# An encoder layer on one core: three side steps a place later, one run of loads on another queue

## The chip, the cores and the metric

The kernel runs on one core of a Trainium2 chip. The metric is the device time of one execution, in microseconds (us). One execution was also recorded by the hardware profiler; its rows give for each instruction the start from the beginning of the span, how long it took and, where the engine stood idle before it, what ended the idle time. PE is the matrix engine, DVE the vector engine, ACT the scalar engine, POOL is GpSimd, and SP is the engine that issues nearly all transfers.

## The reference

```python
mod = jax.nn.silu(c) @ w_ada + b_ada
shift, scale, gate = jnp.split(mod, 3, axis=-1)
h = rmsnorm(x, pre_g) * (1.0 + scale[:, None]) + shift[:, None]
proj = h @ w_in
q, k, v, gate_a, u, gate_p = jnp.split(proj, SPLIT_POINTS, axis=-1)
y_a = windowed_gqa(q, k, v, rel_table, sink) * jax.nn.silu(gate_a)
y_p = multiscale_pool(u, w_pool_grp, pool_scale) * jax.nn.silu(gate_p)
g_a, g_p = jnp.split(jax.nn.sigmoid(h @ w_merge + b_merge), N_BRANCHES, axis=-1)
merged = g_a * (y_a @ w_br_attn) + g_p * (y_p @ w_br_pool)
x = x + gate[:, None] * rmsnorm(merged @ w_out, post_g)
```

x has 1024 rows of 2048 values, w_in is 2048 x 4608, w_merge 2048 x 4096, both branch weights 1024 x 2048, w_out 2048 x 2048; everything is 32-bit floating point.

## The kernel before, in words

**Products.** Each 32-bit operand is split into a high part, which ACT copies (`whi` for weights, line 96), and a low part, which DVE subtracts (`wlo`, line 97). A product is three matmul passes: high by high, high by low, low by high. The big matrix products go through `strassen`: a pair of 128 output rows by 1024 tokens is computed with seven such products of sums of blocks, into three PSUM banks X, Z and V, in the order X<-B11, V<-T3, Z<-T2, X<-B21, V<-T4, Z<-T1, Z<-B22. B11, T3, T2, B21, T4, T1, B22 are seven prepared forms of the moving operand. Between the products ACT copies X into the next Z (line 285), copies Z out as u4 (line 302) and X or Z as c (line 320), and DVE prepares the next weights: sums of blocks of `raw` (lines 114, 117), and `ws`.

**Pairs and side steps.** `run` takes a pair through its seven pieces and, behind some of them, takes one step off a queue `side`. All that is not the main product is such a step: column sums for the modulation, norms, loads and transposes of x, the gate, the pooling, preparation of the next operand. `strassen` is a generator, and the end of a pair (its Z<-B22) is run inside the next pair (`late`, `flush`). The weights `raw` of a pair are loaded about a pair ahead. The order in which an engine takes its instructions follows from the order in which the steps are written, save where a scheduler moves one; `keep` fixes an instruction in the order.

**The four places.**

- *Ramp, from 85 to 112 us.* `modulation(3, …)` sums the fourth group of modulation columns: four steps of GEMV matmuls, whose result ACT copies into `acc` (line 519); a fifth step, `columns`, transposes `acc` with four matmuls into the bank PM (line 480), which DVE reduces (line 482) and turns into `modc` (lines 487, 490). With `modc` ACT and DVE modulate the tiles xT (lines 567, 568) that the next moving operands are made of. `late_sums` says at which of thirteen side steps which of these five are done.
- *Gate, near 529 us.* `gate_sum` loads 32 tiles of w_ada and DVE adds them, weighted, to `gacc` (line 536). `gate_row` sums `gacc` over the partitions by matmuls into the bank GATE (line 885), DVE adds and multiplies (lines 114, 891), and GpSimd stores the row to `pg_d` (line 893). It is the last step of that queue.
- *Right half of x, from 560 to 635 us.* `x_step(n)` loads tile n of 16 (`fetch_x`, line 961, four buffers `xt`), which ACT multiplies in place by the row's factor `rstd` (line 962); at odd n the two tiles of pair (n−3)/2 are transposed by PE (line 968) and copied out by ACT (line 971).
- *Attention's rows for the branch, from 1390 to 1470 us.* `y_steps` loads 16 tiles of `ya_d` (line 1245), one a side step, and then makes sums of them on DVE (`pre`). Beside them the pairs of the projection go on, with `raw` (line 197), `part` loads (line 219) and stores (line 325) all on SP.

```python
late_sums = {0: group2[:1], 4: group2[1:4], 5: group2[4:], 10: group3[:4], 11: group3[4:]}
side = deque(lambda n=n: unit_step(n) for n in range(len(units) + AHEAD))
side.append(gate_row)
```

Of the kernel before, what the change touches and what calls it, by code (L numbers as in the profile page):

```python
# [15 lines left out]
AF = mybir.ActivationFunctionType  # L16
# [14 lines left out]
NB = S // P  # L31
# [12 lines left out]
def encoder_layer(ctx: ExitStack, tc: tile.TileContext, x, c, table, w_ada, b_ada, pre_g,  # L44
# [15 lines left out]
    nc = tc.nc  # L60
# [16 lines left out]
    def uid(s):  # L77
        cnt[0] += 1
        return f"{s}_{cnt[0]}"
# [11 lines left out]
    def keep(ins):  # L91

        tc.keep_in_program_order(ins)
# [25 lines left out]
    load = nc.sync.dma_start  # L119
# [10 lines left out]
    rstd = const.tile([P, NB], F32, name="rstd")  # L130
# [9 lines left out]
    ya_d = dram.tile([NH * P, S], F32, name="ya_d")  # L140
# [16 lines left out]
    def pre_op(j, h1, h2, tmp, pin=lambda ins: None):  # L157

        pin(sub(h1[j][1], h1[j][1], h1[j][0]))
        t2 = tmp()  # L160
        pin(sub(t2, h2[j][1], h1[j][1]))
        return t2
# [198 lines left out]
    held = ExitStack()  # L361
# [4 lines left out]
    for r0, src in ((0, c[0]), (16, b_ada[0, 0:D]), (32, b_ada[0, D:2 * D]),  # L366
                    (48, pre_g[0]), (64, b_merge[0]), (96, pool_scale[0])):
        n = src.shape[0] // P
# [133 lines left out]
    def modulation(j, tile_of, pin=False, apart=False):  # L502

        st_ = {}

        def step(q, between=None):
            if q == 0:
                st_["pv"] = bank("at", "GEMV")
            pv = st_["pv"]
            for kc in range(4 * q, 4 * q + 4):  # L510
                g = kc % 4 * 32
                ins = nc.tensor.matmul(pv[g:g + 32, :], scz[:, kc, :], tile_of(kc), start=kc < 4,
                                       stop=kc >= 12, tile_position=(0, g))
                if pin:
                    tc.keep_in_program_order(ins)
            if q == 3:
                acc = xa2.tile([P, 4, P], F32, tag="acc", name=uid("acc"), bufs=2)
                tc.keep_in_program_order(
                    nc.scalar.activation(acc, pv.rearrange("p (g n) -> p g n", g=4), AF.Copy))
                if between:  # L520
                    between()
                st_["acc"] = acc
                if not apart:
                    columns()

        def columns():
            mod_columns(j, sum_columns(st_["acc"]))

        return [partial(step, q) for q in range(4)] + [columns]
# [134 lines left out]

    group2 = modulation(2, ada[2].__getitem__, True, True)
    group3 = modulation(3, ada3.__getitem__, True, True)
    late_sums = {0: group2[:1], 4: group2[1:4], 5: group2[4:], 10: group3[:4], 11: group3[4:]}
    side = deque((lambda n=n: [step() for step in late_sums.get(n, ())]) for n in range(13))
    for s in range(2):
        for si in range(4 * s, 4 * s + 4):  # L670
# [249 lines left out]
    def unit_step(n):  # L920
        m = n - AHEAD
        if m in then:
            then[m]()
        if m >= 0:
            units[m][1]()
        if n < len(units):
            units[n][0]()

    side = deque(lambda n=n: unit_step(n) for n in range(len(units) + AHEAD))
    side.append(gate_row)  # L930
    EASY = ((0, 2, 4, 6), (1, 3, 5))
    n1 = 20
    sums = deque(weight_sums(j, h_) for h_ in range(2) for j in range(KT // 2))
# [24 lines left out]
    def fetch_x(si, q):  # L958
        xt = xin.tile([P, 512], F32, tag="xt2", name=uid("xt"))
        c0 = 1024 + q * 512  # L960
        load(xt, x[si * P:(si + 1) * P, c0:c0 + 512])
        nc.scalar.activation(xt, xt, AF.Copy, scale=rstd[:, si:si + 1])
        return xt

    def turn_x(si, q, xt):
        pt = bank("sc")
        for j in range(4):
            nc.tensor.transpose(pt[:, j * P:(j + 1) * P], xt[:, j * P:(j + 1) * P], ident)
        for j in range(4):
            dst = h[8 + q * 4 + j][si // 4][:, (si % 4) * P:(si % 4 + 1) * P]  # L970
            nc.scalar.activation(dst, pt[:, j * P:(j + 1) * P], AF.Copy)

    held = {}

    def x_step(n):
        if n < 2 * NB:
            held[n] = fetch_x(n // 2, n % 2)
        if n >= 3 and n % 2:
            for q in range(2):
                turn_x((n - 3) // 2, q, held.pop(n - 3 + q))  # L980

    side = deque(lambda n=n: x_step(n) for n in range(2 * NB + 2))
    side.extend(lambda k=k, s=s: modulate((nc.scalar, nc.vector)[s], h[k][s], k) for k in PART[1] for s in range(2))
    h1, h2, t2 = {j: h[8 + 2 * j] for j in range(4)}, {j: h[9 + 2 * j] for j in range(4)}, {}
# [15 lines left out]
    side = deque()  # L1000
# [12 lines left out]
    with pool("attn") as ap:  # L1013
# [116 lines left out]
        def step(u, e):  # L1130
            nu = len(UNITS)
            if e == 0 and 0 <= u - LAG_V < nu:
                values(u - LAG_V)
            if e == 1 and u % 16 in (1, 3) and u < nu:
                turn_v(u % 16 // 2)
            if e == 1 and 0 <= u - LAG_T < nu:
                turn(u - LAG_T, 0)
                turn(u - LAG_T, 1)
            if u < nu:
                if u % 16 == 0 and e == 0:  # L1140
                    take_k(UNITS[u][0] * 2 // GQA)
                if u % 4 == 0:
                    split_q(e)
                scores(u, e)
            if e == 1:
                if opened:
                    gated(*opened.pop())
                if u % 4 == 3 and u + 1 < nu:
                    fetch_q(u + 1)
                c_ = u - LAG_V + 1  # L1150
                if (c_ + 1) % 16 == 0 and c_ + 1 < nu:
                    fetch_v(UNITS[c_ + 1][0] * 2 // GQA)
                if 0 <= c_ < nu:
                    if c_ % 4 == 0:
                        fetch_gate(c_)
# [83 lines left out]
    ysrc = ExitStack()  # L1239
    sp = ysrc.enter_context(pool("ysrc"))  # L1240

    def y_steps(yd, store_to):
        def get(k, s):
            t = sp.tile([P, 512], F32, tag="y", name=uid("y"), bufs=16)
            load(t, yd[k * P:(k + 1) * P, s * 512:(s + 1) * 512])
            h1, h2, _ = store_to
            (h1 if k < 4 else h2).setdefault(k % 4, []).append(t)

        def pre(j):
            h1, h2, t2 = store_to  # L1250
            t2[j] = pre_op(j, h1, h2, lambda: sp.tile([P, 512], F32, tag="tf", name=uid("tf"), bufs=4), keep)

        return [lambda k=k, s=s: get(k, s) for k in (0, 4, 1, 5, 2, 6, 3, 7) for s in range(2)] + \
            [lambda j=j: pre(j) for j in range(4)]

    ys = [({}, {}, {}), ({}, {}, {})]
    side.extend(y_steps(ya_d, ys[0]))
    while side:
        next_pair(range(7))
    while pidx[0] < PAIRS:  # L1260
# [22 lines left out]
    for b, w in enumerate((w_ba, w_bp)):  # L1283
        op = new_op()
        fill_op(op, range(4), *ys[b], now=7 if b else 3)
        if b == 0:
            side.extend(y_steps(yp_d, ys[1]))
        else:
            ysrc.close()
            ev_ctx.close()  # L1290
            ev_ctx = ExitStack()
            ev = ctx.enter_context(pool("ev4", 4, side="right"))
            mr = ctx.enter_context(pool("mraw", side="right"))

            def merged_tiles():

                return [[mr.tile([P, 2, 512], F32, tag="m", name=uid("m"), bufs=2 * JP) for _ in range(JP)]
                        for _ in range(2)]

            def merged_sums(m, t2, jp):  # L1300

                b12 = m[0][jp][:, :, 256:512]
                keep(sub(b12, b12, m[0][jp][:, :, 0:256]))
                t2[jp] = mr.tile([P, 2, 256], F32, tag="t2", name=uid("t2"), bufs=JP)
                keep(sub(t2[jp], m[1][jp][:, :, 256:512], b12))

            mt, mt2 = merged_tiles(), {}
            side.extend([lambda: None] * 25)
            for jp in range(JP - 1):
                side[6 * jp + 7] = lambda jp=jp: merged_sums(mt, mt2, jp)  # L1310
# [86 lines left out]
    xrow, held = {}, {}  # L1397
# [159 lines left out]
    side = deque()  # L1557
# [128 lines left out]
```

## Time and profile before

| | us |
|---|---|
| median of three runs | 2106.81 (2106.34 to 2109.77) |
| profiled execution | 2109.9 |
| its span | 2107.8 |
| PE busy | 2076.6 |
| DVE busy | 1539.0 |
| ACT busy | 1106.5 |
| GpSimd busy | 25.5 |

The span is what the profiler's rows cover; 2.1 us of the execution lie around it. PE is busy for 99% of the span, at a granted clock of 0.998. A row of a timeline stands for one instruction or for several alike that follow each other (x4); matmuls overlap, so that a group's time reaches past the start of the next. What tells whether PE stood idle is the distance of two starts.

### The profile page before, as it was taken

Reading aid. Unit: us, or ns where it says so; the run is one execution under the profiler, and the core shown is the slowest. Engines: PE = TensorE matmul, PEld = TensorE weight load, DVE = VectorE, ACT = ScalarE, POOL = GpSimd, SP = SyncE. Lnnn points to the kernel's source line nnn. Section 1 sums busy time; section 2 is a strip of 40 time slices with the busy share of each in tenths; the row PEclk is TensorE's granted clock in tenths of the full one; section 3 lists DMA queues with packets and bytes.
Section 4 is the critical chain, followed back from the end, with each engine's and each line's share of the span. In section 5 each row is a group of like instructions: output and inputs, shape, how many; then the busy total and the mean of one; then the engine's idle time right before and its main releaser. Section 6 shows DMA issues by size and latency. Waiting matters only on the chain.

```text
span 2107.8 us, 28866 instructions
## 1 busy us (share of the span) xinstructions
PE 2076.6 (99%) x9511; PEld 1707.8 (81%) x9511; DVE 1539.0 (73%) x2769; ACT 1106.5 (52%) x2105; POOL 25.5 (1%) x103
## 2 busy tenths in 40 slices
PE   6999999999999999999999999999999999999998
PEld 4688888888788888888888888888788788888886
DVE  5886777777547766677777688856857977889667
ACT  4754444444464635566665443333645644767555
POOL 0000000000000000000000000000000000000000
PEclk9999999999999999999999999999999999999999
DMA  9888688887666455454554577665745566686997
GB/s 323 293 271 273 222 271 285 269 286 241 205 220 212 137 184 188 160 173 160 183 164 154 163 243 221 218 212 192 250 158 173 175 196 200 217 314 206 292 330 251
DMA packets 303273, 468.18 MB, mean 222 GB/s; under 512 B 23939, under 2 KB 144875, under 8 KB 303124
## 3 DMA queue, kind: packets, MB, share of 16 engines
q1 hardware_dynamic: 299328, 457.79, 66.6%
q0 software_dynamic: 2336, 6.33, 0.8%
q10 hardware_dynamic: 1460, 2.22, 0.3%
q8 instruction: 74, 1.21, 0.2%
q14 instruction: 75, 0.61, 0.1%
HBM read 341.45 MB, written 126.90 MB: 222 GB/s over the span
## 4 chain that ended last, share of the span: by engine, by line
PE 90%; DMA 5%; DVE 3%; ACT 1%; issue 1%; SPq 0%; DVEq 0%; ACTq 0%
PE Z L247 30%; PE V L247 20%; PE X L247 20%; PE Z L1393 2%; PE Z L1395 2%; PE Z L1394 2%; DMA ada<-in_w_ada_dram 2%; PE X L1395 1%; PE X L1393 1%; PE X L1394 1%; PE V L1395 1%; PE V L1394 1%; PE V L1393 1%; PE PT L1103 1%; DMA xt<-in_x_dram 1%; DMA raw<-in_w_merge_dram 1%
## 5 line engine op out<-in xcount | busy, mean ns | idle before, releaser
L96 ACT ACTIVATE whi<-raw 128x512 fp32r<-128x512 f32 (+1 forms) x532 | 321.5, 606 | 510.7 <-PE Z L247 256.1
L97 DVE TENSOR_TENSOR wlo<-raw,whi 128x512 fp32r<-128x512 f32 (+1 forms) x532 | 346.9, 657 | 164.1 <-PE Z L247 122.3
L97 DVE TENSOR_TENSOR wlo<-wr,whi 128x512 fp32r<-128x512 f32 x224 | 150.5, 689 | 51.4 <-ACT whi L96 48.3
L96 ACT ACTIVATE whi<-wr 128x512 fp32r<-128x512 f32 x224 | 138.1, 629 | 87.9 <-DVE wlo L97 28.0
L114 DVE TENSOR_TENSOR raw<-raw,raw 128x512 f32<-128x512 f32 x79 | 54.5, 690 | 83.9 <-DMA raw<-in_w_merge_dram 61.7
L247 PE MATMUL X<-B11h,whi 128*128 128x512 f32 x334 | 90.8, 390 | 1.4 <-ACT c L320 1.4
L247 PE MATMUL V<-T3h,whi 128*128 128x512 f32 x334 | 90.8, 391 | 1.1 <-DVE u L114 1.1
L96 ACT ACTIVATE whi<-ws 128x512 fp32r<-128x512 f32 (+1 forms) x88 | 53.7, 610 | 72.2 <-PE X L247 65.7
L247 PE MATMUL Z<-B22h,whi 128*128 128x512 f32 x334 | 91.0, 392 | 0.0
L247 PE MATMUL Z<-T1h,whi 128*128 128x512 f32 x334 | 90.9, 390 | 0.0
L247 PE MATMUL X<-B21h,whi 128*128 128x512 f32 x334 | 90.7, 391 | 0.0
L247 PE MATMUL V<-T4l,whi 128*128 128x512 f32 x334 | 90.6, 390 | 0.1
L247 PE MATMUL V<-T4h,whi 128*128 128x512 f32 x334 | 90.6, 391 | 0.0
L247 PE MATMUL Z<-T2h,whi 128*128 128x512 f32 x334 | 90.3, 390 | 0.3 <-ACT whi L96 0.2
L247 PE MATMUL Z<-T2h,wlo 128*128 128x512 f32 x334 | 90.3, 390 | 0.3 <-DVE wlo L97 0.3
L247 PE MATMUL X<-B11l,whi 128*128 128x512 f32 x334 | 90.4, 390 | 0.0
L247 PE MATMUL Z<-T1l,whi 128*128 128x512 f32 x334 | 90.4, 390 | 0.0
L247 PE MATMUL Z<-B22l,whi 128*128 128x512 f32 x334 | 90.3, 390 | 0.0
L247 PE MATMUL Z<-B22h,wlo 128*128 128x512 f32 x334 | 90.2, 390 | 0.1
L247 PE MATMUL V<-T3l,whi 128*128 128x512 f32 x334 | 90.2, 390 | 0.0
L247 PE MATMUL X<-B21l,whi 128*128 128x512 f32 x334 | 90.2, 390 | 0.0
L247 PE MATMUL Z<-T1h,wlo 128*128 128x512 f32 x334 | 90.2, 390 | 0.0
(363 smaller groups left out, 4811.6 us busy)
## 6 DMA issues: line engine op xcount, KB each, us to landing
part<-part_d SPq DMA_DIRECT2D x136, 256.0 KB, 4.8
ada<-in_w_ada_dram SPq DMA_DIRECT2D x128, 256.0 KB, 5.6
raw<-in_w_merge_dram SPq DMA_DIRECT2D x64, 512.0 KB, 5.5
raw<-in_w_in_dram SPq DMA_DIRECT2D x62, 512.0 KB, 4.1
wr<-ws_dS SPq DMA_DIRECT2D x60, 512.0 KB, 5.3
wr<-in_w_out_dram SPq DMA_DIRECT2D x48, 512.0 KB, 5.1
proj_d<-part SPq DMA_DIRECT2D x68, 256.0 KB, 2.2
sw<-in_w_out_dram SPq DMA_DIRECT2D x64, 256.0 KB, 5.8
```

What stands on the lines that cost most here:

```text
L96: ins = (nc.scalar.activation(hi, src, AF.Copy), nc.vector.tensor_tensor(lo, src, f32(hi), ALU.subtract))
L97: nc.vector.tensor_tensor(lo, src, f32(hi), ALU.subtract))
L114: return (eng or nc.vector).tensor_tensor(o, a, b, ALU.add)
L247: nc.tensor.matmul(ps, w_[:, i], op[mov][j][m_], start=fresh and i == 0 and n == 0, stop=i == nj - 1 and n == 2, skip_group_check=True)
L1103: nc.tensor.transpose(pt[:, i * P:(i + 1) * P], p[:, i * P:(i + 1) * P], ident)
L1393: nc.tensor.matmul(pb, hi, w[0], start=first, stop=False, skip_group_check=True)
L1394: nc.tensor.matmul(pb, lo, w[0], start=False, stop=False, skip_group_check=True)
L1395: nc.tensor.matmul(pb, hi, w[1], start=False, stop=last, skip_group_check=True)
```

## The change

Four edits. The transposes and sums of the fourth modulation group (`group3[4:]`) go from side step 11 to 12. `gate_row` goes one side step back, behind an empty one. The scaling of x's tile n−1 by its row factors is issued in step n, behind the load of tile n, and fixed in the order with `keep`; before it stood directly behind its own load. The 16 loads of `ya_d` are issued by GpSimd instead of SP; the later loads of `yp_d` stay on SP.

```diff
-    late_sums = {0: group2[:1], 4: group2[1:4], 5: group2[4:], 10: group3[:4], 11: group3[4:]}
+    late_sums = {0: group2[:1], 4: group2[1:4], 5: group2[4:], 10: group3[:4], 12: group3[4:]}
...
-    side.append(gate_row)
+    side.extend((lambda: None, gate_row))
...
         load(xt, x[si * P:(si + 1) * P, c0:c0 + 512])
-        nc.scalar.activation(xt, xt, AF.Copy, scale=rstd[:, si:si + 1])
         return xt
...
             held[n] = fetch_x(n // 2, n % 2)
+        if 0 < n <= 2 * NB:
+            keep(nc.scalar.activation(held[n - 1], held[n - 1], AF.Copy, scale=rstd[:, (n - 1) // 2:(n - 1) // 2 + 1]))
...
-    def y_steps(yd, store_to):
+    def y_steps(yd, store_to, load=load):
...
-    side.extend(y_steps(ya_d, ys[0]))
+    side.extend(y_steps(ya_d, ys[0], nc.gpsimd.dma_start))
```

On ACT in the ramp, before (`acc_257` is the sum of the fourth group, `modc` the modulation, `u4_267` the copy of Z that frees the bank for Z<-B22, the line 285 copy starts the next Z):

```order
L519 ACTIVATE acc_257_1009<-GEMV_256_992 128x512
L96 ACTIVATE B22h_336_1306<-xT_13_161 128x512
L96 ACTIVATE whi_274_1076<-ws_273_1074 128x256
L320 ACTIVATE c_260_1021<-X_241_937 128x512
L96 ACTIVATE whi_277_1088<-raw_81_302 128x256
L567 ACTIVATE xT_8_149<-xT_8_149,modc_79 128x512
L567 ACTIVATE xT7_0_151<-xT7_0_151,modc_79 128x512
L96 ACTIVATE whi_280_1103<-raw_126_393 128x256
L302 ACTIVATE u4_267_1056<-Z_242_938 128x512
L96 ACTIVATE B11h_338_1314<-xT_8_149 128x512
L96 ACTIVATE whi_283_1115<-raw_126_393 128x256
L285 ACTIVATE Z_269_1061<-X_268_1060 128x512
```

The same place after:

```order
L519 ACTIVATE acc_257_1009<-GEMV_256_992 128x512
L96 ACTIVATE B22h_336_1306<-xT_13_161 128x512
L96 ACTIVATE whi_274_1076<-ws_273_1074 128x256
L320 ACTIVATE c_260_1021<-X_241_937 128x512
L96 ACTIVATE whi_277_1088<-raw_81_302 128x256
L96 ACTIVATE whi_280_1103<-raw_126_393 128x256
L567 ACTIVATE xT_8_149<-xT_8_149,modc_79 128x512
L302 ACTIVATE u4_267_1056<-Z_242_938 128x512
L96 ACTIVATE whi_283_1115<-raw_126_393 128x256
L567 ACTIVATE xT7_0_151<-xT7_0_151,modc_79 128x512
L285 ACTIVATE Z_269_1061<-X_268_1060 128x512
```

One modulation now stands ahead of u4 instead of two, and one more weight part stands ahead of the modulations. On PE the four transposes into PM stood between X<-B21 and V<-T4 of that pair; now they stand between V<-T4 and Z<-T1. On DVE the reduction of PM, which stood ahead of `ws` and of the addition u<-V, stands behind both. Nothing else moves in the ramp on PE.

On ACT in the right half of x, before (`xt_1161` and `xt_1167` are tiles 8 and 9 of 16, the pair that PE transposes behind the end of that pair's Z<-T2; `xt_1179` and `xt_1187` are tiles 10 and 11):

```order
L962 ACTIVATE xt_1161_5560<-xt_1161_5560,rstd_80 128x512
L962 ACTIVATE xt_1167_5587<-xt_1167_5587,rstd_80 128x512
L96 ACTIVATE whi_1180_5660<-raw_1144_5454 128x512
L302 ACTIVATE u4_1160_5556<-Z_1125_5360 128x512
...
L257 ACTIVATE p7_1173_5626<-V_1164_5565 128x512
L962 ACTIVATE xt_1179_5655<-xt_1179_5655,rstd_80 128x512
L567 ACTIVATE h10_0_5183<-h10_0_5183,modc_79 128x512
L962 ACTIVATE xt_1187_5686<-xt_1187_5686,rstd_80 128x512
L96 ACTIVATE whi_1196_5748<-raw_1144_5454 128x512
L320 ACTIVATE c_1176_5644<-Z_1125_5360 128x512
```

The same place after:

```order
L302 ACTIVATE u4_1160_5555<-Z_1125_5359 128x512
L978 ACTIVATE xt_1153_5500<-xt_1153_5500,rstd_80 128x512
...
L285 ACTIVATE Z_1163_5563<-X_1162_5562 128x512
L978 ACTIVATE xt_1161_5559<-xt_1161_5559,rstd_80 128x512
...
L257 ACTIVATE p7_1173_5625<-V_1164_5564 128x512
L567 ACTIVATE h10_0_5183<-h10_0_5183,modc_79 128x512
L978 ACTIVATE xt_1187_5685<-xt_1187_5685,rstd_80 128x512
L96 ACTIVATE whi_1196_5747<-raw_1144_5453 128x512
L320 ACTIVATE c_1176_5643<-Z_1125_5359 128x512
L978 ACTIVATE xt_1167_5586<-xt_1167_5586,rstd_80 128x512
```

The scalings of tiles 8 and 9 leave their place ahead of u4; tile 8 comes behind the line 285 copy, tile 9 behind tile 11, two tiles out of turn. The loads on SP keep their order there.

On SP near 1400 us, before (`raw_2726` is the second half of the next pair's weights, `y` the loads of `ya_d`):

```order
L197 DMA raw_2725_13642<-in_w_merge_dram 128x4x256
L1221 DMA yp_d_91<-sil7_13270 128x1024
L1245 DMA y_2702_13512<-ya_d_90 128x512
L1245 DMA y_2707_13534<-ya_d_90 128x512
L1245 DMA y_2710_13554<-ya_d_90 128x512
L325 DMA proj_d_89<-part_2666_13318 128x512
L1245 DMA y_2714_13577<-ya_d_90 128x512
L1245 DMA y_2717_13598<-ya_d_90 128x512
L1245 DMA y_2720_13618<-ya_d_90 128x512
L325 DMA proj_d_89<-u2_2683_13416 128x512
...
L197 DMA raw_2726_13644<-in_w_merge_dram 128x4x256
```

The same place after:

```order
L197 DMA raw_2725_13642<-in_w_merge_dram 128x4x256
L1222 DMA yp_d_91<-sil7_13270 128x1024
L325 DMA proj_d_89<-part_2666_13318 128x512
L325 DMA proj_d_89<-u2_2683_13416 128x512
L197 DMA raw_2726_13644<-in_w_merge_dram 128x4x256
L219 DMA part_2693_13484<-part_d_83 128x512
L219 DMA part_2694_13486<-part_d_83 128x512
```

The loads of y are gone from SP and stand, all 16 in a row, at the end of what GpSimd has to issue up to there. `raw_2726` has also moved ahead of four `part` loads and of the store of p7. On DVE the sum that needs `raw_2726` (line 114) moves four places forward, ahead of the weight part `wlo` for X<-B21.

## The prediction

> **What bounds the kernel now.** I read the page's busy times first, then the list of waits with PE as the waiting engine, then the wait of the gate's line, which the list leaves out because it falls inside a group.
>
> ```profile
> PE 2076.6 (99%) x9511; PEld 1707.8 (81%) x9511; DVE 1539.0 (73%) x2769; ACT 1106.5 (52%) x2105; POOL 25.5 (1%) x103
> PE X L247 <- ACT c L320: 1.4, 1, 1.4
> PE V L247 <- DVE u L114: 1.1, 1, 1.1
> PE PM L480 <- ACT acc L519: 1.0, 1, 1.0
>   DVE gacc L536: 0.9, 1
> ```
>
> PE works 99% of the span, and no edit takes a matmul away. So the change can only win back stretches in which PE stood still. The four rows are four such stretches, each met once, and each belongs to one edit. Together they are worth 4 to 5 us of 2107.8; nothing else that the edits touch makes PE wait. Below I measure each from PE's own starts. The pitch of the 512-wide matmuls is 0.227 us (in the rows below four of them take the next group 0.91 us further, two 0.45); a stall is what a distance of starts has beyond that.
>
> **Edit 1, the fourth modulation group (ramp).** Rows of PE, ACT and DVE:
>
> ```profile
> 89.86 0.62 PE L247 MATMUL X<-B21h,wlo 128*128 128x512 f32 x2
> 91.52 0.66 PE L480 MATMUL PM<-ident,acc 128*128 128x128 f32 x4 [1.04 <-ACT acc L519]
> 97.50 0.62 PE L247 MATMUL Z<-B22h,whi 128*128 128x512 f32 x2
> 90.88 0.59 ACT L519 ACTIVATE acc<-GEMV 128x512 f32<-128x512 f32 x1
> 94.29 0.15 DVE L490 SCALAR_TENSOR_TENSOR modc<-modc,cols 128x2 f32<-128x2 f32 x1
> 96.22 0.57 ACT L302 ACTIVATE u<-Z 128x512 f32<-128x512 f32 x1
> 97.52 0.58 ACT L285 ACTIVATE Z<-X 128x512 f32<-128x512 f32 x1
> ```
>
> Two matmuls from 89.86 end their turn at 90.32; the transposes begin at 91.52, since `acc` is copied only at 90.88 to 91.47. Stall: 1.20. After the change PE has six matmuls of V<-T4 to do first, 1.36 us, and reaches the transposes at 91.68, behind the copy's end. That stall goes.
>
> What is late next: `modc` was ready at 94.44. The transposes are now done near 92.1, but on DVE the reduction stands behind `ws` and u<-V, and u<-V waits for V<-T4; by the rows of these operations I get `modc` 1.0 us later, near 95.5. ACT has a modulation that needs it, and behind that u4, which frees the bank of Z<-B22. One modulation instead of two stands ahead of u4, so u4 starts at about 96.3, as before (96.22), and ends at 96.87. But PE, 1.20 earlier, is at Z<-B22 at 97.50 − 1.20 = 96.30. It waits 0.57. The other modulation now stands ahead of the copy Z<-X, which moves from 97.52 to about 97.8; Z<-T2 waits for it some 0.17. Left of 1.20: **0.46**. The bounds are 1.20 (u4 and the copy in time) and −0.2 (`modc` another 0.7, one modulation, later).
>
> **Edit 2, the gate.** Rows of PE, of the same operation on another tile too:
>
> ```profile
> 353.37 1.06 PE L885 MATMUL PMR<-acc,onez 128*32 128x512 f32 x8
> 354.36 1.20 PE L247 MATMUL V<-T3h,whi 128*128 128x512 f32 x4
> 529.17 2.11 PE L885 MATMUL GATE<-gacc,onez 128*32 128x512 f32 x8
> 531.21 1.19 PE L247 MATMUL Z<-B22h,whi 128*128 128x512 f32 x4
> ```
>
> The same eight matmuls hold PE for 0.99 us when their inputs are there (PMR) and for 2.04 when they wait for the last sum of `gacc`. They now stand 24 matmuls later, 24 × 0.227 = 5.4 us, when that sum has long ended: gain **1.05**. DVE's two operations on the row and GpSimd's four stores move along; nothing reads the row before the end of the layer. Were the cover gone (an addition on DVE pushed in front of a weight part), it would cost one operation, 0.69 us; I take nothing.
>
> **Edit 3, x's scalings.** The wait of PE, what ACT did then, and the group of the scalings with its waits and the landing times of their loads:
>
> ```profile
> 605.79 1.07 PE L247 MATMUL Z<-T1h,wlo 128*128 128x512 f32 x4
> 608.23 1.19 PE L247 MATMUL X<-B11h,whi 128*128 128x512 f32 x4 [1.36 <-ACT c L320]
> 606.97 0.72 ACT L962 ACTIVATE xt<-xt,rstd 128x512 f32<-128x512 f32 x1 [1.72 <-DMA xt<-in_x_dram]
> 607.60 0.58 ACT L320 ACTIVATE c<-X 128x512 f32<-128x512 f32 x1
>   DMA xt<-in_x_dram: 16.4, 7
> DMA to landing us min/median/max: 3.4/5.1/6.3
> 592.00 0.38 SPq L961 DMA_DIRECT2D xt<-in_x_dram x1
> 597.64 1.03 PE L968 MATMUL b<-ident,xt 128*128 128x128 f32 x8
> ```
>
> ACT stood 16.4 us in seven waits for tiles of x; one of them reached PE. Four matmuls after 605.79 PE wants bank X at 606.70 and starts at 608.23: 1.53 us, because c, which frees X, sat on ACT behind a scaling whose tile landed only at 606.97. With the scalings behind, c goes when X is done. Gain **1.52**.
>
> What is late next: the order puts tile 11 ahead of tile 9, and PE transposes tile 9 with the second four of the eight at 597.64, so at 598.07. Tile 9 is then ready when tile 11 has landed, plus two scalings (0.72 each), a weight part and c between them: about 2.4 us. Tile 11 was issued at 592.00. SP stood there behind the store of p7, which waited for u4, which sat behind two late scalings; without these I estimate the issue at 590.1. With the median landing, 590.1 + 5.1 + 2.4 = 597.6: in time. With the longest, 6.3, it is 598.8, a stall of 0.7; with the issue at 592.00 besides, 2.6. I take 0, the case of the median, and keep 2.6 for the range.
>
> **Edit 4, the loads of y.** SP's issues, what DVE did with the weights that they delayed, PE's rows, and how GpSimd issues a tile of the same size elsewhere:
>
> ```profile
> 1396.12 1.86 SPq L1245 DMA_DIRECT2D y<-ya_d  x3
> 1403.89 0.32 SPq L325 DMA_DIRECT2D proj_d<-u  x1
> 1408.85 0.48 SPq L197 DMA_DIRECT2D raw<-in_w_merge_dram  x1
> 1418.20 0.32 SPq L325 DMA_DIRECT2D proj_d<-part  x1
> 1418.57 1.40 SPq L1245 DMA_DIRECT2D y<-ya_d  x3
> 1420.07 0.38 SPq L197 DMA_DIRECT2D raw<-in_w_merge_dram  x1
> 1416.87 0.69 DVE L114 TENSOR_TENSOR raw<-raw,raw 128x512 f32<-128x512 f32 x1 [4.26 <-DMA raw<-in_w_merge_dram]
> 1427.30 0.69 DVE L117 TENSOR_TENSOR ws<-raw 128x512 f32<-128x512 f32 x1 [5.52 <-DMA raw<-in_w_merge_dram]
> 1427.91 0.68 DVE L114 TENSOR_TENSOR u<-V,u 128x512 f32<-128x512 f32 x1
> 1418.38 1.07 PE L247 MATMUL X<-B21h,wlo 128*128 128x512 f32 x4
> 1426.54 1.07 PE L247 MATMUL X<-B11h,wlo 128*128 128x512 f32 x4
> 1428.74 1.17 PE L247 MATMUL V<-T3h,whi 128*128 128x512 f32 x4 [1.13 <-DVE u L114]
> L117 DVE TENSOR_TENSOR y<-y,y x4: 682/684/691, 1454.6 to 1464.9; 128x512 f32<-128x512 f32 x4
> L1509 POOL DMA_DIRECT2D o_d<-c x2: 552/570/587, 1838.1 to 1839.9; - x2
> o_d<-c POOLq DMA_DIRECT2D x2, 256.0 KB, 6.5
> 1390.00:1430.00 40.00, 38.87 (x172) 31.85 (x171) 20.34 (x33) 11.78 (x19) 0.00 (x0) 1.00 0.74 237
> ```
>
> V<-T3 should start at 1427.45 and starts at 1428.74: 1.29 us. V's bank is freed by u<-V on DVE, which stood behind `ws`, which waited until 1427.30 for a load issued at 1420.07. Three loads of y stand between that load and the store at 1418.20; without them it goes out by 1418.6, at least 1.5 us sooner, and the store itself was late behind DVE's wait of 4.26. So `ws` is ready 1.5 us or more sooner, which covers 1.29. Gain **1.29**.
>
> A new wait stands on DVE: the sum of raw_2726 now comes ahead of the weight part that PE wants at 1418.38 for X<-B21, so whatever is queued behind it waits for that load. Its issue moves from 1408.85 to just behind the store at 1403.89, near 1404.4. It took until 1416.87, 8 us, with loads of y around it; with 8 us again it lands at 1412.4, still 6 us ahead of 1418.38. The weight part takes 0.69 and sits one place behind the sum, so landings up to about 1417 cost nothing.
>
> GpSimd has nothing else to do there. Sixteen issues at 0.57 are 9 us; 16 × 256 KB at the window's 237 GB/s are 17.7 us, so from 1396.1 the last lands near 1414 plus one landing of 6.5, far ahead of 1464.9, when the last sum of y is made. Where DMA's share (0.74) has no room for more, the burst lands on raw_2726. The Trainium skill ("DMA: Bandwidth & Descriptors", section "SWDGE vs HWDGE vs iDMA") says that each DMA engine takes the software and the hardware queue in turn, and gives plain transfers to SP or ACT; by it y does not leave raw_2726's way when it leaves SP, and the gain would be in the issue alone. No row here has both queues under load; the worst of it is the second rival.
>
> **Sum.** 0.46 + 1.05 + 1.52 + 1.29 = 4.32 us. The profiled execution would go from 2109.9 (span 2107.8 and 2.1 around it) to 2105.6, the median from 2106.81 to **2102.5**. Every gap of the four taken whole is 1.20 + 1.05 + 1.52 + 1.29 = 5.06. That the profiled execution is 3.1 above the median is a doubt: two of the stalls hang on landing times and may be smaller in the other executions.
>
> **Rivals.**
>
> *Tile 9 late, or the ramp's stall merely moved.* For it: the order on ACT. Against it: the median landing. Tile 9 costs 0.7 to 2.6, the ramp at its lower bound another 0.66. Gain 1.5 to 3.5: 2103.3 to 2105.3. Chance 0.21.
>
> *raw_2726 in the burst.* Sixteen tiles queued at once by about 1405 ahead of it: if it waits for all of them (1413.8) and then its 8 us, it lands near 1421.8, and PE, wanting its weight part at 1418.38, stands 4.8 us; the gain of 4.32 is used up: 2107.3. Half of that delay costs about 0.4. Chance 0.07, most of it near 2104.
>
> *Stalls of the profiled run.* The landings of edits 3 and 4 were unlucky; then those two terms are halved: gain 2.9, 2103.9. Chance 0.14.
>
> *Slower: GpSimd's queue carries one load at a time.* Sixteen at 6.5 us end at 1396.1 + 104 = 1500, 35 us behind the last sum of y. DVE takes these sums in order, so it holds the weights too, and PE starves: 2102.5 + 35 = 2138. It decides from (1464.9 − 1396.1) / 16 = 4.3 us a load. Against it: the two o_d stores are issued 1.8 us apart with landings of 6.5, so two are under way at once. The Trainium skill ("SBUF — State Buffer", "two separate sides") tells of a GpSimd transfer that takes 3.1 us instead of 0.62 while DVE copies, since GpSimd writes its descriptors; by it the last lands at 1446, under the point. Chance 0.06, and 0.05 more for a smaller hold-up of this kind, since no row shows more than two loads of this size on that queue at once.
>
> *The change doesn't do what it says:* the scalings are out of turn already, so one could again stand in front of c; this lies in the first rival's range.
>
> **How the numbers follow.** 0.2% is 4.2 us, about what a measurement of this kernel can tell from no change. The forecast, 4.3 with 0.6 either way, has 0.47: 0.29 of it beyond 4.2, and the rest within. On top of the gaps counted, freed queues may ease others: of the third rival's and the first's chance 0.13 comes out beyond 4.2 by that. So faster 0.42, slower 0.12 (the fourth rival with the tail of the second), within 0.46. The range runs from 2101.0 (the lowest run, 2106.34, less 5.06, and 0.3 for what else is eased) to 2106.3 (the first rival's worst, 2105.3, and half of what the second adds).
>
> **What would show it.** Right: the waits of PE for `acc`, c and u gone from the list, the eight matmuls of the gate in 0.99 us, transposes of tile 9 without idle time, raw_2726 landed before 1417. Wrong: a wait of PE for the copy u4 over 1 us near 95, for a scaling near 597, for a weight part near 1415, or DVE waiting for y at 1455.

## The result, and the profile after

The changed kernel takes 2103.79 us, the median of 15 runs (2101.49 to 2105.27), beside 2107.36 us (15 runs) of the kernel before. The ratio is 0.9981 with a 95% interval of 0.9974 to 0.9988. By the ratio that is 4.0 us less, between 2.5 and 5.5; the two medians themselves differ by 3.6. Forecast were 4.3. The two profiled executions differ by more, spans of 2107.8 and 2099.7, but they are one of the longer runs of the one kernel (2109.9) and the fastest of the other (2101.49); so the profiles are compared place by place here, and the total is taken from the 15 runs of each.

The list of waits of PE after the change, from the first row past the start-up on. None of the three waits that stood in the list before is left, and no new one of their size has come:

```profile
PE PB L696 <- ACT B11h L567: 1.2, 2, 0.7
PE Z L247 <- DVE wlo L97: 0.2, 1, 0.2
PE PV L1115 <- DVE pp L97: 0.2, 1, 0.2
PE Z L247 <- ACT whi L96: 0.2, 1, 0.2
```

Timelines of PE, ACT and DVE in the ramp:

```profile
89.97 0.62 PE L247 MATMUL X<-B21h,wlo 128*128 128x512 f32 x2
91.79 0.60 PE L480 MATMUL PM<-ident,acc 128*128 128x128 f32 x4
96.36 0.62 PE L247 MATMUL Z<-B22h,whi 128*128 128x512 f32 x2
89.92 0.59 ACT L519 ACTIVATE acc<-GEMV 128x512 f32<-128x512 f32 x1
95.46 0.58 ACT L302 ACTIVATE u<-Z 128x512 f32<-128x512 f32 x1
94.54 0.16 DVE L490 SCALAR_TENSOR_TENSOR modc<-modc,cols 128x2 f32<-128x2 f32 x1
```

Six matmuls of V<-T4 lie between the first two rows, and the transposes begin when they are through: no wait. But `acc` was copied at 89.92 here, 0.96 earlier than in the profile before, while PE was at the same point within 0.11. From 86 to 92 us every row of ACT is ahead by that much in this execution; just before, ACT had waited 1.68 us for a transfer (`ramp_d<-c`), and in the profile before 2.74 us. So u4 ends at 96.04, ahead of Z<-B22 at 96.36, and the wait of 0.57 that I forecast there isn't in this profile. Whether that is the rule is a matter of the experiments.

The gate, PE:

```profile
533.47 1.06 PE L885 MATMUL GATE<-gacc,onez 128*32 128x512 f32 x8
534.46 1.20 PE L247 MATMUL X<-B21h,whi 128*128 128x512 f32 x4
```

The eight matmuls hold PE for 0.99 us, as those of PMR do. Right half of x: SP's load of tile 11, ACT's scalings of tiles 11 and 9, PE's transposes of tiles 8 and 9, and ACT's waits for tiles (the row of the tile's view):

```profile
587.92 0.38 SPq L961 DMA_DIRECT2D xt<-in_x_dram  x1
593.76 0.72 ACT L978 ACTIVATE xt<-xt,rstd 128x512 f32<-128x512 f32 x1 [1.53 <-DMA xt<-in_x_dram]
595.39 0.71 ACT L978 ACTIVATE xt<-xt,rstd 128x512 f32<-128x512 f32 x1
595.44 1.36 PE L967 MATMUL b<-ident,xt 128*128 128x128 f32 x8
596.56 1.17 PE L247 MATMUL X<-B21h,whi 128*128 128x512 f32 x4
  DMA xt<-in_x_dram: 1.5, 1
```

ACT's waits for x have gone from 16.4 us in seven to 1.5 in one, and that one is the tile out of turn. Tile 11 lands 5.84 us behind its issue, tile 9 is ready at 596.10, and the transposes hold PE for 1.12 us (595.44 to 596.56) where they took 0.79 before (597.64 to 598.43): a new wait of 0.33.

Attention's rows: SP's weight loads, what DVE made of them, PE at the weight part that had become the point at risk, and GpSimd's loads of y:

```profile
1400.36 0.38 SPq L197 DMA_DIRECT2D raw<-in_w_merge_dram  x1
1415.03 0.38 SPq L197 DMA_DIRECT2D raw<-in_w_merge_dram  x1
1410.59 0.69 DVE L114 TENSOR_TENSOR raw<-raw,raw 128x512 f32<-128x512 f32 x1 [7.46 <-DMA raw<-in_w_merge_dram]
1411.19 0.68 DVE L97 TENSOR_TENSOR wlo<-raw,whi 128x512 fp32r<-128x512 f32 x1
1419.60 0.69 DVE L117 TENSOR_TENSOR ws<-raw 128x512 f32<-128x512 f32 x1 [1.59 <-DMA raw<-in_w_merge_dram]
1414.26 1.07 PE L247 MATMUL X<-B21h,wlo 128*128 128x512 f32 x4
1423.33 1.07 PE L247 MATMUL V<-T3h,whi 128*128 128x512 f32 x4
L1246 POOL DMA_DIRECT2D y<-ya_d x16: 536/536/586, 1382.8 to 1402.5; - x16
```

The second load goes out at 1415.03 and `ws` starts at 1419.60, 3.73 us ahead of V<-T3; before it was 1.44 ahead, and late. The load itself took 4.6 us, where it took 7.2 before (1420.07 to 1427.30): SP had then issued three loads of y just ahead of it and two behind it, while here GpSimd had issued its last one by 1402.5. The first load took 10.2 us (1400.36 to 1410.59), not 8, and DVE stood 7.46 us for it. The weight part behind it was ready at 1411.87, 2.4 us before PE wanted it. GpSimd issued all 16 loads at 0.54 us each.

### The profile page after: what moved, and what is told of

It reads as the page before. It is cut to its first block, busy times and chain, and to the rows that moved or that the text cites. A ratio compares the mean times of both kernels' runs of the same rounds, so it can differ in the third digit from the quotient of the medians.

```text
span 2099.7 us, 28891 instructions
## 1 busy us (share of the span) xinstructions
PE 2073.3 (99%) x9511; PEld 1709.1 (81%) x9511; DVE 1540.1 (73%) x2769; ACT 1108.6 (53%) x2105; POOL 33.9 (2%) x119
## 4 chain that ended last, share of the span: by engine, by line
PE 94%; DVE 1%; DMA 1%; ACT 0%; issue 0%; DVEq 0%; SPq 0%; ACTq 0%
PE Z L247 32%; PE X L247 21%; PE V L247 21%; PE Z L1394 2%; PE Z L1396 2%; PE Z L1395 2%; PE X L1396 1%; PE V L1396 1%; PE V L1394 1%; PE X L1394 1%; PE X L1395 1%; PE V L1395 1%; PE PT L1104 1%; PE PV L1115 0%; PE PV L1116 0%; PE PV L1114 0%
## 5 line engine op out<-in xcount | busy, mean ns | idle before, releaser
L247 PE MATMUL V<-T3h,wlo 128*128 128x512 f32 x334 | 90.1, 389 | 0.0
```

The source lines that it names most:

```text
L247: nc.tensor.matmul(ps, w_[:, i], op[mov][j][m_], start=fresh and i == 0 and n == 0, stop=i == nj - 1 and n == 2, skip_group_check=True)
```

## The experiments

Twelve profiled executions now show the same places, ten of them with three or more of the edits in. This table is worked out from PE's starts, as in the prediction: what a distance is beyond the pitch, "–" for under 0.1. Column "x tile 9" is the time from the first of the eight transposes to the next product beyond 0.79; "1490–1512" is the sum of the gaps over 0.15 there.

| kernel | acc, 90 | u4, 96 | GATE − 0.99 | c, 606 | x tile 9 | u, 1427 | 1490–1512 |
|---|---|---|---|---|---|---|---|
| before | 1.20 | – | 1.05 | 1.53 | – | 1.29 | 1.15 |
| before again | – | – | 0.79 | 0.43 | – | 1.38 | 1.08 |
| changed | – | – | – | – | 0.33 | – | – |
| changed again | – | – | – | – | 0.33 | – | – |
| group as before | 0.64 | – | – | – | 0.44 | – | – |
| gate as before | – | – | 0.93 | – | 0.79 | – | – |
| scalings as before | – | 0.29 | – | 2.03 | – | – | – |
| y on SP | – | – | – | – | 0.54 | 1.41 | 1.32 |
| tiles in turn | – | 0.13 | – | – | – | – | – |
| y on ACT | – | – | – | – | 1.50 | – | – |
| y loaded twice | – | 0.43 | – | – | – | – | 1.98 |
| in turn, and ACT | – | – | – | – | – | – | – |

The last column leaves out the smaller delays between those gaps. Taken from start to start, over the same matmuls from one V<-T3 to the Z<-T2 behind the next, the stretch is whole. First with y on SP, then in the changed kernel:

```profile
1483.90 1.07 PE L247 MATMUL V<-T3h,whi 128*128 128x512 f32 x4
1508.29 1.08 PE L247 MATMUL Z<-T2l,whi 128*128 128x512 f32 x4
1483.25 1.07 PE L247 MATMUL V<-T3h,whi 128*128 128x512 f32 x4
1505.92 1.07 PE L247 MATMUL Z<-T2l,whi 128*128 128x512 f32 x4
```

It lasts 24.39 us with y on SP (24.41 and 24.38 in the two profiles of the kernel before), 22.67 in all eight executions with y elsewhere and loaded once, and 25.54 with y loaded twice. So y on SP costs 1.7 us there, and the same each time.

The ratios below have intervals of about 1.9 us to either side, and that of every version overlaps the changed kernel's. By its time alone none of them is told from the changed kernel; the sizes come from the rows, of one execution each.

Each experiment below starts from the changed kernel, save the one that is the kernel before.

**The group as before.**

```diff
-    late_sums = {..., 10: group3[:4], 12: group3[4:]}
+    late_sums = {..., 10: group3[:4], 11: group3[4:]}
```

> The changed kernel with the fourth group's transposes back at side step 11; the other three edits stay. Theory (each stall belongs to its edit alone): PE waits for acc again, 0.2 to 1.2 us near 90, and no other of the four waits comes back; time 0.5 to 1.2 us above the changed kernel's, about 0.9985 of the kernel before. Rival (the ramp's gain of 1.2 is given back by waits for u4 and Z<-X): same time as the changed kernel within 0.3 us.

Measured: 2103.28 us, ratio 0.9979 (0.9970 to 0.9988). PE's timeline:

```profile
90.11 0.66 PE L480 MATMUL PM<-ident,acc 128*128 128x128 f32 x4 [0.48 <-ACT acc L519]
```

The wait for `acc` is back, 0.64 by the starts, and no other of the four. The time was expected 0.5 to 1.2 us above the changed kernel's; by the ratios it is 0.4 below, but the times can't tell a difference of this size. So edit 1 takes away a wait, but one that differs from execution to execution, as the second profile of the kernel before shows more sharply.

**The gate as before.**

```diff
-    side.extend((lambda: None, gate_row))
+    side.append(gate_row)
```

> The changed kernel with the gate's row one side step earlier, as before. Theory: the eight GATE matmuls hold PE for 2.0 us instead of 1.0, nothing else changes, time 1.05 us above the changed kernel's (0.9986 of before). Rival (the wait for gacc was an accident of the profiled run): GATE holds PE for 1.0 us here too.

Measured: 2104.16 us, ratio 0.9985 (0.9976 to 0.9994). PE's timeline:

```profile
529.57 1.99 PE L885 MATMUL GATE<-gacc,onez 128*32 128x512 f32 x8
531.49 1.20 PE L247 MATMUL Z<-B22h,whi 128*128 128x512 f32 x4
```

GATE holds PE for 1.92 us again. The wait was 1.05, 0.79 and 0.93 us in the three executions with the gate at its old place, and there was none in the nine others.

**The scalings as before.**

```diff
         load(xt, x[si * P:(si + 1) * P, c0:c0 + 512])
+        nc.scalar.activation(xt, xt, AF.Copy, scale=rstd[:, si:si + 1])
...
-        if 0 < n <= 2 * NB:
-            keep(nc.scalar.activation(held[n - 1], held[n - 1], ...))
```

> The changed kernel with each scaling of x directly behind its load again. Theory: ACT waits some 16 us for tiles of x, PE waits for c near 604 for about 1.5 us, and the small wait of PE for tile 9 (0.4 us in the profile of the changed kernel) goes: time 1.1 us above the changed kernel's. Rival (the landing at 607 was unlucky): PE's wait for c is under 0.5 us.

Measured: 2104.05 us, ratio 0.9983 (0.9974 to 0.9991). PE and ACT:

```profile
607.04 1.20 PE L247 MATMUL X<-B11h,whi 128*128 128x512 f32 x4 [1.87 <-ACT c L320]
605.78 0.72 ACT L962 ACTIVATE xt<-xt,rstd 128x512 f32<-128x512 f32 x1 [1.66 <-DMA xt<-in_x_dram]
```

The wait for c is back, 2.03 us, behind a scaling that waits for its tile, and the one at tile 9 is gone. The mechanism is as told; its size follows the landing.

**y on SP.**

```diff
-    side.extend(y_steps(ya_d, ys[0], nc.gpsimd.dma_start))
+    side.extend(y_steps(ya_d, ys[0]))
```

> The changed kernel with the 16 loads of y on SP again. Theory: the second weight load (raw_2759) goes out 1.5 to 3 us later behind loads of y, ws is late, PE waits for u near 1423 for about 1.3 us; time 1.3 us above the changed kernel's. Rival (unlucky landing): wait under 0.5 us. If leaving SP also eased later places, PE's small gaps at 1490 to 1510 (1.2 us together before) come back too, and the time is 2.5 us above.

Measured: 2104.84 us, ratio 0.9988 (0.9979 to 0.9997). PE at the old place and at a later one, then DVE's first sums of y:

```profile
1423.88 1.15 PE L247 MATMUL V<-T3h,whi 128*128 128x512 f32 x4 [1.25 <-DVE u L114]
1494.17 1.10 PE L247 MATMUL V<-T4l,whi 128*128 128x512 f32 x2 [0.57 <-DVE T4l L97]
L117 DVE TENSOR_TENSOR y<-y,y x4: 681/685/689, 1450.5 to 1460.8; 128x512 f32<-128x512 f32 x4
```

Both come back: 1.41 at 1423 and 1.32 in all from 1490 to 1512 (1.7 with the smaller delays). The second was not in the prediction. To see where it comes from, take DVE alone in the window 40 us long behind V<-T3, of the kernel before, of this one and of the changed one (columns: window, length, busy, instructions, clock, DMA share, GB/s):

```profile
1430.00:1470.00 40.00, 28.17 (x47) 1.00 0.58 181
1425.00:1465.00 40.00, 27.43 (x45) 1.00 0.56 176
1425.00:1465.00 40.00, 30.29 (x50) 1.00 0.58 191
```

With y on SP, DVE gets 45 to 47 operations done where it gets 50 done without: it idles more, waiting for weights. Then it is full, in the kernel before

```profile
1470.00:1500.00 30.00, 29.97 (x51) 1.00 0.68 221
```

without a gap, and carries its lateness to the operands of the branch. It has next to no room there to make up what it lost: in the 30 us that start 41 us behind V<-T3 it is busy for 29.97 in all three executions with y on SP, and for 29.7 in the eight with y elsewhere and loaded once. One weight load that DVE waits for, its issue by SP and the end of DVE's wait, with y on SP and then in the changed kernel, whose row of the sums of y stands last:

```profile
1442.19 0.38 SPq L197 DMA_DIRECT2D raw<-in_w_merge_dram  x1
1448.53 0.69 DVE L114 TENSOR_TENSOR raw<-raw,raw 128x512 f32<-128x512 f32 x1 [5.17 <-DMA raw<-in_w_merge_dram]
1438.69 0.38 SPq L197 DMA_DIRECT2D raw<-in_w_merge_dram  x1
1444.87 0.69 DVE L114 TENSOR_TENSOR raw<-raw,raw 128x512 f32<-128x512 f32 x1 [3.66 <-DMA raw<-in_w_merge_dram]
L117 DVE TENSOR_TENSOR y<-y,y x4: 681/684/687, 1446.8 to 1457.2; 128x512 f32<-128x512 f32 x4
```

The load takes the same time in both, 6.3 and 6.2 us, and y has long left SP (its last issue is at 1417). It goes out 3.5 us later, 2.9 of them beyond the difference of the two kernels at V<-T3 (1423.88 and 1423.33), since it waits for a buffer that DVE, late itself, frees: the delay is handed from pair to pair. The first sum of y comes 26.6 us behind V<-T3 in this kernel and 23.5 in the changed one; 25.9 and 26.1 in the two profiles of the kernel before, 23.1 to 23.8 in the seven other executions with y off SP and loaded once. So edit 4 is worth what I counted, 1.3 to 1.4, and 1.7 more some 65 us later.

**Tiles in turn.**

```diff
-            keep(nc.scalar.activation(held[n - 1], held[n - 1], ...))
+            with behind("scaled"):
+                anchor["scaled"] = nc.scalar.activation(held[n - 1], held[n - 1], ...)
+            keep(anchor["scaled"])
```

Each scaling is tied behind the one before, so tile 9 comes ahead of tiles 10 and 11.

> The changed kernel with the scalings of x tied to the order of their loads, so that tile 9 no longer stands behind tile 11. Theory: the small wait of PE inside the transposes of tile 9 (0.2 to 0.6 us in the profiles so far, with the four matmuls' own pitch 0.4 in the changed kernel) is gone, nothing else moves; time 0.4 us below the changed kernel's, 0.9979 of before. Rival (the wait is of the transposes themselves): it stays.

Measured: 2102.44 us, ratio 0.9977 (0.9968 to 0.9986). ACT's scaling of tile 9, and PE:

```profile
593.59 0.79 ACT L979 ACTIVATE xt<-xt,rstd 128x512 f32<-128x512 f32 x1
595.28 1.03 PE L967 MATMUL b<-ident,xt 128*128 128x128 f32 x8
596.07 1.17 PE L247 MATMUL X<-B21h,whi 128*128 128x512 f32 x4
```

Tile 9 is ready at 594.38, 0.9 us before PE begins the pair, and the transposes take 0.79. The wait was that of the order, as the first rival had it.

**y on ACT.**

```diff
-    side.extend(y_steps(ya_d, ys[0], nc.gpsimd.dma_start))
+    side.extend(y_steps(ya_d, ys[0], nc.scalar.dma_start))
```

> The changed kernel with the 16 loads of y issued by ACT. Theory A (what counts is that y no longer stands in SP's queue ahead of the weight loads): PE's wait for u near 1423 stays away, and so do the small gaps from 1490 to 1512, as with GpSimd; the time is that of the changed kernel within 0.5 us, plus what 16 issues cost on ACT (some 0.4 us each, off the path). Theory B (the software queue gives way to the hardware queues): raw_2726 takes clearly longer than the 10.2 us it took in the changed kernel, over 13 us, and PE waits at X<-B21 near 1414 for 1 us or more.

Measured: 2102.77 us, ratio 0.9980 (0.9971 to 0.9989). DVE's sum that waits for raw_2726 (issued at 1401.50), then ACT's scaling of tile 11, which stands ahead of tile 9's, and PE's transposes of tile 9:

```profile
1409.19 0.69 DVE L114 TENSOR_TENSOR raw<-raw,raw 128x512 f32<-128x512 f32 x1 [4.93 <-DMA raw<-in_w_merge_dram]
594.83 0.73 ACT L978 ACTIVATE xt<-xt,rstd 128x512 f32<-128x512 f32 x1 [2.71 <-DMA xt<-in_x_dram]
597.22 0.66 PE L967 MATMUL b<-ident,xt 128*128 128x128 f32 x4 [1.28 <-ACT xt L978]
```

No wait at 1427 or from 1490 on, as with GpSimd: what counts is that y leaves SP's queue, not which queue it goes to. That is theory A. Theory B is wrong in its direction too: it had raw_2726 take longer than the 10.2 us of the changed kernel, and it takes 7.7, and neither reaches PE. That the kind of queue makes this difference is not shown, since ACT issued its loads of y from 1394.8 to 1414.5 and GpSimd from 1382.8 to 1402.5, so that raw_2726 met another part of the burst. The edit doesn't touch x, yet in this execution tile 11 landed late (6.6 us behind its issue at 588.22), and tile 9, behind it on ACT, kept PE waiting for 1.50: the new order's risk at its largest.

**y loaded twice.**

```diff
             load(t, yd[k * P:(k + 1) * P, s * 512:(s + 1) * 512])
+            if yd is ya_d:
+                load(t, yd[k * P:(k + 1) * P, s * 512:(s + 1) * 512])
```

> The changed kernel with each of the 16 loads of y done twice by GpSimd, 8.4 MB instead of 4.2. Theory (the burst shares the DMA engines with the weights, and only the landing of raw_2726 before 1417 matters): the burst lasts past 1425, raw_2726 lands within 2 us of where it did (1410.6), or later by up to 5 us; if it lands past about 1414 PE waits for the weight part of X<-B21. The sums of y at 1447 are still in time. Rival (GpSimd's queue takes one load at a time): 32 landings of 6 us reach 1580 and PE stands for over 50 us.

Measured in one run: 2106.49 us. GpSimd's first and second loads, DVE's sums of y, and PE later:

```profile
L1246 POOL DMA_DIRECT2D y<-ya_d x16: 536/536/586, 1384.6 to 1423.0; - x16
L1248 POOL DMA_DIRECT2D y<-ya_d x16: 536/536/538, 1394.1 to 1430.5; - x16
L117 DVE TENSOR_TENSOR y<-y,y x4: 680/682/684, 1452.5 to 1462.8; 128x512 f32<-128x512 f32 x4
1494.38 0.50 PE L247 MATMUL V<-T4h,whi 128*128 128x512 f32 x1 [0.49 <-ACT T4h L96]
```

GpSimd had issued 32 loads by 1431; one at a time at 6 us would have reached 1580. In ten waits, 21.0 us in all, the second load of a tile stood until the first had landed. The rival that ended slower falls. The Trainium skill gives in "SBUF — State Buffer", section "two separate sides", 3.1 us for a transfer of this kind that overlaps a DVE `tensor_copy`. That case was not met here: from 1382 to 1432 DVE ran tensor_tensor and scalar_tensor_tensor alone, and the issues took 0.54 each. raw_2726 landed where the theory had it (1411.9), but the sums of y were not in time: the first came at 1452.5, not 1447. The wait for u stays away, but DVE, which waited longer for the next pairs' weights, is later than with y on SP (its first sum of y comes 27.4 us behind V<-T3), and the gaps from 1490 on come back with 1.98. It is the same cost by another cause: lateness of DVE, not the place of y in a queue.

**The kernel before, again.** Nothing is changed.

> The kernel before, profiled once more, to see how much its four stalls differ between executions. Theory: the stall for acc lies between 0.2 and 1.2 us, GATE holds PE 2.0 us, the wait for c is 1 to 2 us, that for u 0.8 to 1.5 us, and the gaps from 1490 to 1512 add to about 1.2 us. Rival (stalls of the one profiled execution): at least one of c and u is under 0.3 us.

Measured in one run: 2110.50 us. PE's timeline in the ramp and two rows of its waits:

```profile
92.44 0.60 PE L480 MATMUL PM<-ident,acc 128*128 128x128 f32 x4
PE X L247 <- ACT c L320: 0.3, 1, 0.3
PE V L247 <- DVE u L114: 1.5, 2, 1.2
```

Neither theory nor rival holds as written. GATE (0.79), u and the late gaps are near those of the first profile. The wait for `acc` isn't there at all, and that for c is 0.43 by the starts instead of 1.53: below the theory's 1 to 2, above the rival's 0.3. These two stalls belong to an execution as much as to the kernel.

**Tiles in turn and y on ACT; the changed kernel again.** The first joins the two edits shown above.

> The changed kernel with the scalings of x in the order of their loads and the loads of y issued by ACT, the two versions that each left fewer waits of PE. Theory: no wait of PE at tile 9, raw_2726 lands 7.7 us behind its issue instead of some 10, no wait of PE near 1423 or 1490; time 0.4 to 1.3 us below the changed kernel's (what tile 9 cost in the profiles), 0.9975 of before. Rival: with 16 issues among its weight parts ACT is late somewhere and the time is that of the changed kernel or above.

> The changed kernel once more, beside the version with tiles in turn and y on ACT on the same chip. Theory: 0.998 of before; PE's wait at tile 9 lies between 0.2 and 1.4 us, the gaps at 90, 529, 607, 1423 and 1490 to 1512 stay away, and raw_2726 lands 9 to 11 us behind its issue. Rival: one of the four stalls is back, so that the edit only made it rarer.

Measured: 2102.91 us, ratio 0.9976 (0.9966 to 0.9986), and 2103.43 us, ratio 0.9981 (0.9972 to 0.9990). The first has none of the waits of the table; the second is like the first profile of the changed kernel, tile 9 included. The joined version is clearly faster than the kernel before. Against the changed kernel it is 1 us ahead by the ratios and 0.5 by the two medians, with intervals that overlap, so a gain is not shown. Putting tiles in turn takes out a wait that every profile with tile 9 behind tile 11 but one has.

## Why the prediction was right, and where not

The total was right: 4.3 forecast, 4.0 (2.5 to 5.5) measured. Of its terms one was right, and of the other three one was too small and two were taken from an execution that showed them large. The misses cancel, and that the total came this close is in part luck.

- **Edit 1 (0.46).** The wait for `acc` goes. Its size in three executions with the old place is 1.20, 0.64 and none, 0.6 on the mean, not 1.20. The wait for u4 that I set against it was worked out for ACT as late as in that one profile. It appears with 0.29, 0.43 and 0.13 in three of nine executions with the new place, and the 0.17 at Z<-T2 in none. The net of some 0.5 is near the forecast, by sizes that were all too large.
- **Edit 2 (1.05).** 1.05, 0.79, 0.93: right. The row's operations on DVE and GpSimd show in no wait of PE.
- **Edit 3 (1.52).** The mechanism is right; the size is 1.53, 0.43 and 2.03, 1.3 on the mean. The step that failed is "I take 0" at tile 9. The chain I gave was right link by link: the issue estimated at 590.1, found at 587.92 with PE 2.2 earlier by then (transposes at 595.44 for 597.64); 2.34 us from landing to ready, for 2.4. Only the landing was 5.84, where I had taken the median of 5.1. Over seven executions with that order the wait is 0 to 1.50, 0.56 on the mean. So the net is nearer 0.8.
- **Edit 4 (1.29).** The step that failed is the sentence that nothing else the edits touch makes PE wait. The wait for u was 1.29 to 1.41 and is gone. But the stretch from 1488 to 1513 lost 1.7 us with it, since DVE is full there and carries what it lost earlier. I had its gaps only as rows under 0.4 each, and did not reckon with DVE's 29.97 busy of 30. The term is about 3.1. The way to `ws` was half right too: I had its load go out 1.5 us sooner and take as long as before. Measured from the moment PE wants V<-T3, with y on GpSimd and loaded once, it went out 0.9 to 2.1 us sooner and took 4.5 to 4.9 us in place of 7.0 to 7.2, so that more of the gain came from the shorter load in all six of these executions.
- **raw_2726.** The new wait on DVE is there, longer than forecast (10.2 us for 8) and harmless, as the slack of some 5 us said. The Trainium skill ("DMA: Bandwidth & Descriptors", section "SWDGE vs HWDGE vs iDMA") has each DMA engine take the two kinds of queue in turn. By that y stays in the weights' way wherever it is issued, and for raw_2726 the trace doesn't speak against it: the load took 8.0 to 8.4 us with y on SP, 9.4 to 10.2 with y on GpSimd, 7.7 and 7.8 on ACT. That the gain would be in the issue alone fails at the second load, the one that `ws` waits for. It took 7.0 to 7.2 with y on SP, 4.5 to 4.9 with y on GpSimd, whose last load of y had gone out some 12 us before, and 6.0 and 6.9 with y on ACT, whose last went out at 1414.5, beside it. Off SP, the burst of y was over sooner.
- **Rivals.** The first (tile 9 late) happened in part, with 0.3 to 1.5. The third (the landings of edits 3 and 4 were unlucky) is right in part for edit 3 and wrong for edit 4, whose wait for u came in all three executions with y on SP; it fits edit 1, which it didn't name. The second and the fourth didn't happen. GpSimd issued y not from 1396.1 on, as I had reckoned, but from 1382.8; 12 of the 16 loads had gone out when raw_2726 was issued.

By these means the terms would be 0.5 + 0.9 + 0.8 + 3.1 = 5.3, near the upper end of the interval. What makes the difference to the measured 4.0 stays open.

## What to carry to other kernels

A stall read from one profile may have the size of that execution: the wait for `acc` was 1.20, 0.64 and none, that for c 1.53, 0.43 and 2.03. Others come back at nearly the same size each time, here the gate's row (0.79 to 1.05) and the wait for u (1.29 to 1.41), though a landing ends the latter. A second profile tells the two kinds apart, before a stall is counted whole. When an engine that the bound engine waits for is full for tens of microseconds, as DVE was here, its idle time ahead of that stretch can be on the path: the loads that made it wait were paid twice, once at once and once where its lateness came out. And where scalings or copies are moved behind their loads, look at the order in which they come out; one tile out of turn gave back up to the whole gain.

## What the runs showed of the hardware

A weight load of 512 KB beside sixteen loads of 256 KB took 9.4 to 10.2 us when these went through GpSimd's queue, 8.0 to 8.4 when they stood around it on SP, and 7.7 and 7.8 when ACT issued them; when the loads went out differed too. The next load of weights took 7.0 to 7.2 us with loads of y issued around it on SP, and 4.5 to 4.9 when GpSimd had issued its last one some 12 us before. GpSimd needed 0.54 us for an issue, SP 0.44, ACT 0.35 (medians). Thirty-two such loads went through GpSimd's queue in 46 us with landings of 3.9 to 9.3, ten of them held until the load before of the same tile had landed.
